# All 512 value columns of retention head 0 in the opening, in eight PSUM banks

## The chip, the cores and the metric

The kernel runs on one core of a Trainium2 chip. A core has TensorE (PE, matrix products into eight PSUM banks of 128 partitions by 512 float32), VectorE (DVE), ScalarE (ACT), GpSimd (POOL) and the queues that issue loads and stores (here mostly that of SyncE, SP). The metric is the device time of one execution in microseconds (us), the median of several runs. Before the change it was 1136.06 us, the median of three runs from 1134.89 to 1136.76.

## What is computed

One block of a hybrid model, for 512 tokens of width 1024: a normalised and modulated input `hmix` is projected by `w_in` into the inputs of two mixers (stick-breaking attention with 16 heads, retention with 4 heads), both are gated, projected and merged, and a gated feed-forward layer follows. What matters here is the beginning:

```python
mod = jnp.einsum('bd,de->be', c_act, w_ada[l]) + b_ada[l]
shift1, scale1, gate1, shift2, scale2, gate2 = jnp.split(mod, N_MOD, axis=-1)
hmix = modulate(rmsnorm(x, g_norm1[l]), shift1, scale1)
proj = jnp.einsum('bsd,de->bse', hmix, w_in[l])
sb_q, sb_k, sb_v, r_q, r_k, r_v, r_g, br = jnp.split(proj, IN_SPLITS, axis=-1)
...
rq = rotary(r_q.reshape(b, s_len, RET_HEADS, RET_QK_DIM))
rk = rotary(r_k.reshape(b, s_len, RET_HEADS, RET_QK_DIM)) * (RET_QK_DIM ** -0.5)
rv = r_v.reshape(b, s_len, RET_HEADS, RET_V_DIM)
o_ret = retention(rq.transpose(0, 2, 1, 3), rk.transpose(0, 2, 1, 3), rv.transpose(0, 2, 1, 3))
o_ret = head_rmsnorm(o_ret.transpose(0, 2, 1, 3)).reshape(b, s_len, RET_V_WIDTH)
o_ret = jax.nn.silu(r_g) * o_ret
```

A retention head has 256 query columns, 256 key columns, 512 value columns and 512 gate columns.

## The kernel before, in words

Products are made in three passes: every float32 operand is split into a high part (ScalarE copies it with rounding) and a low part (VectorE subtracts the high part), and a product is high by high, high by low and low by high, added up in one bank. `split` does this, `weight` loads a block of weights and splits it, `mm` (line 230) records every product, so nearly all rows of TensorE have that line.

The first part of the program, the **opening**, is written out in its order for PE, DVE and ACT; the queues and GpSimd stay with the scheduler, and so does everything between the opening and later written-out parts: there a scheduler with a cost model of its own puts instructions in order, and names (`ps_218`) are given anew at each build. The opening does this:

- `c` is activated and spread over all partitions by eight products (banks `z`); `keep_busy` issues products of a constant that nobody reads (`negones`, lines 456 to 464). The eight x tiles (128 rows of the width each) are squared, seven by ACT and one by DVE, and DVE adds squares 1 to 5 to square 0 (line 480). PE sums the columns of square 0 (with its additions), 6 and 7 in two halves of 256 tokens (`ssq`), and from these `rsqrt_rows` makes the factor r1, half by half.
- The modulation columns of tile n come from two loads of 512 KB (`sraw`), each multiplied by `cact` and summed by DVE (`dot`, line 391); the first shift column comes from PE (`dot_pe`). `h_t` (L429, DVE), `h_hi` (L435, ACT) and `h_lo` (L438, DVE) make the modulated tile n in high and low part.
- For tile n a `start` weight is loaded: its 128 rows, 256 query, 256 key and 256 value columns of head 0 (384 KB), split by `w_hi` (L418, ACT) and `w_lo` (L422, DVE). Tile 0 is multiplied unsplit, in plain float32 and in halves. Tiles 1 to 7 take 12 products of 512 columns for queries and keys (banks `ps` three times and `av`, with the weight as the stationary operand) and 12 of 256 columns for values (two blocks of 128 tokens share a bank `z`, so two banks).

After the opening `ret_qk` rotates queries and keys (L676 to L678, four reads of banks on DVE for each), `ret_v` splits the first half of the values, then `ret_scores` makes the scores from rotated queries and keys into three banks `z`; then `tok_proj` makes the other 256 value columns, with two weights of 512 KB and 96 products of 256 columns into two banks `ps`, and `ret_v` splits them. `ret_silu` makes the gate columns of head 0 with `tok_proj_wide`: four weights of 512 KB and 96 products of 512 columns into four banks `ps`. `ret_out` multiplies scores and values (30 products), squares the result, and `ret_gate` scales it and transposes it (L787). While this runs, DVE makes sums of the modulated tiles that later products need (`sv_acts`, L895 and L906).

The PSUM banks are four of the name `ps`, three `z` and one `av`. Weights have three buffers for what is loaded (`raw`), four for high parts (`whi`, of which `cact` holds one during the opening) and four for low parts (`wlo`).

## Time and profile before

| | |
|---|---|
| median of three runs | 1136.06 us (1134.89 to 1136.76) |
| the profiled execution | 1136.24 us, with a span of 1134.2 us from the first to the last instruction |
| PE busy | 1115.5 us, 98% of the span |
| DVE, ACT, GpSimd busy | 839.7, 554.6 and 55.3 us |
| first tile of the opening starts | 16.72 us |
| first product of the separate value half behind the opening | 53.41 us |
| gate columns of head 0, first to last product | 69.07 to 90.64 us |
| bytes moved, whole span | 190.92 MB |

The rows are read like this: start in us, duration in us, engine, source line, operation, what is written from what, shapes, count. In rows of the chain of waits only start, duration, engine, tile and line stand. Products overlap, so their durations are longer than the distance of their starts, and the distance is what counts for a sum. A plain float32 product leaves two records.

### The profile page before, as it was taken

To read this page: it belongs to the slowest core of one execution; us is meant where nothing else is said; L and a number is where in the kernel's file an instruction comes from. 1 tells how busy PE (TensorE), PEld (TensorE's weight loads), DVE (VectorE), ACT (ScalarE), POOL (GpSimd) and SP (SyncE) were. 2 spreads that over 40 slices of the span, in tenths; PEclk is the share of its full clock that TensorE was granted. 3 is DMA by queue.
4 is the path that set the end of the run, shared out by engine and by line. 5 is a ranking of instruction groups with operands and counts; after the bars stand their busy time and mean duration, and the time that the engine had idled before them with its cause. 6 is when DMAs were issued, how large, how long until landed. Compare 5 with 4: busy or idle time off the path is not lost.

```text
span 1134.2 us, 16143 instructions
## 1 busy us (share of the span) xinstructions
PE 1115.5 (98%) x6196; PEld 965.4 (85%) x6196; DVE 839.7 (74%) x1181; ACT 554.6 (49%) x869; POOL 55.3 (5%) x94
## 2 busy tenths in 40 slices
PE   8999999999999999999999999999999999999996
PEld 7888888888788888877878777889999999999986
DVE  7997846958977968377677756767997677677656
ACT  5445345445444645355565554357755444444333
POOL 0000000011021020000000000000000000000000
PEclk9999999999999999999999999999999999999998
DMA  9724341766776476866676348762565653565322
GB/s 352 281 75 149 130 130 60 234 134 204 241 167 206 152 157 226 219 193 180 170 203 169 119 139 279 264 186 56 150 185 152 184 168 107 148 181 141 93 75 75
DMA packets 63437, 190.92 MB, mean 168 GB/s; under 512 B 7809, under 2 KB 9857, under 8 KB 63361
## 3 DMA queue, kind: packets, MB, share of 16 engines
q1 hardware_dynamic: 56048, 171.02, 46.9%
q0 software_dynamic: 6768, 18.35, 9.5%
q8 instruction: 49, 0.80, 0.3%
q10 hardware_dynamic: 544, 0.52, 0.1%
q14 instruction: 28, 0.22, 0.1%
HBM read 146.35 MB, written 16.78 MB: 144 GB/s over the span
## 4 chain that ended last, share of the span: by engine, by line
PE 82%; DVE 7%; DMA 4%; ACT 4%; issue 2%; SPq 0%; DVEq 0%; ACTq 0%
PE ps L230 63%; PE z L230 14%; PE av L230 3%; DMA araw<-wada 3%; PE z L638 2%; DVE araw L258 2%; ACT s L622 1%; DVE wlo L876 1%; DVE wlo L210 1%; ACT g L825 1%; DVE t L783 0%; DMA t<-t 0%; PE z L787 0%; DMA o<-xT 0%; DVE s L211 0%
## 5 line engine op out<-in xcount | busy, mean ns | idle before, releaser
L230 PE MATMUL ps<-h,whi 128*128 128x512 f32 (+1 forms) x1154 | 340.0, 376 | 0.2
L230 PEld LDWEIGHTS ps<-h,whi 128*128 128x128 f32 x1154 | 208.1, 189 | 34.9 <-ACT h L435 1.6
L230 PE MATMUL ps<-h,wlo 128*128 128x512 f32 (+1 forms) x577 | 214.8, 376 | 0.0
L208 ACT ACTIVATE whi<-raw 128x1024 fp32r<-128x1024 f32 (+1 forms) x106 | 110.7, 1044 | 179.3 <-PE ps L230 127.7
L210 DVE TENSOR_TENSOR wlo<-raw,whi 128x1024 fp32r<-128x1024 f32 (+1 forms) x106 | 127.3, 1202 | 68.3 <-ACT whi L208 67.7
L230 PE MATMUL ps<-s,whi 128*128 128x512 f32 x480 | 148.7, 390 | 1.1 <-ACT s L208 0.9
L230 PEld LDWEIGHTS ps<-h,wlo 128*128 128x128 f32 x577 | 108.9, 189 | 17.2
L230 PE MATMUL z<-q,whi 128*128 128x256 f32 x504 | 106.8, 283 | 0.0
L230 PEld LDWEIGHTS ps<-s,whi 128*128 128x128 f32 x480 | 89.3, 188 | 19.8 <-ACT s L208 1.3
L876 DVE TENSOR_TENSOR wlo<-s,whi 128x1024 fp32r<-128x1024 f32 x46 | 56.3, 1225 | 53.8 <-ACT whi L872 53.7
L230 PE MATMUL ps<-s,wlo 128*128 128x512 f32 x240 | 93.4, 389 | 0.0
L230 PEld LDWEIGHTS z<-q,whi 128*128 128x128 f32 x504 | 84.9, 192 | 1.5
L230 PE MATMUL ps<-whi,h 128*128 128x512 f32 (+1 forms) x272 | 77.9, 365 | 0.0
L872 ACT ACTIVATE whi<-s 128x1024 fp32r<-128x1024 f32 x47 | 49.7, 1057 | 56.9 <-PE ps L230 41.8
L1185 DVE SCALAR_TENSOR_TENSOR o<-ps,mod,o 128x512 f32<-128x512 f32 (+1 forms) x63 | 42.4, 680 | 30.8 <-PE ps L230 30.8
L230 PEld LDWEIGHTS ps<-whi,h 128*128 128x128 f32 x272 | 49.2, 189 | 9.2 <-ACT t L1016 0.6
L210 DVE TENSOR_TENSOR s<-z,s 128x512 fp32r<-128x512 f32 (+1 forms) x60 | 33.6, 613 | 28.8 <-ACT s L208 28.8
L230 PEld LDWEIGHTS ps<-s,wlo 128*128 128x128 f32 x240 | 45.1, 188 | 9.4
L872 ACT ACTIVATE whi<-raw 128x1024 fp32r<-128x1024 f32 x28 | 29.6, 1058 | 43.9 <-PE ps L230 42.1
L230 PE MATMUL ps<-wlo,h 128*128 128x512 f32 (+1 forms) x136 | 49.5, 364 | 0.0
L230 PE MATMUL ps<-q,whi 128*128 128x256 f32 (+1 forms) x224 | 49.3, 314 | 0.0
L230 PE MATMUL z<-qp,whi 128*128 128x256 f32 x168 | 47.2, 283 | 0.0
(318 smaller groups left out, 2116.9 us busy)
## 6 DMA issues: line engine op xcount, KB each, us to landing
raw<-wp SPq DMA_DIRECT2D x139, 512.0 KB, 4.1
araw<-wada SPq DMA_DIRECT2D x32, 512.0 KB, 4.2
araw<-wp SPq DMA_DIRECT2D x30, 512.0 KB, 4.8
s<-wp SPq DMA_DIRECT2D x24, 512.0 KB, 5.8
sraw<-wada SPq DMA_DIRECT2D x16, 512.0 KB, 7.8
q<-qp SPq DMA_DIRECT2D x32, 256.0 KB, 3.7
spill<-o POOLq DMA_DIRECT2D x24, 256.0 KB, 4.7
o<-xT SPq DMA_DIRECT2D x16, 256.0 KB, 4.4
```

The costliest lines, as they stand in the source:

```text
L208: nc.scalar.activation(dst_hi, src, AF.Copy, scale=scale)
L210: return (eng or nc.vector).tensor_sub(dst_lo, src, f(dst_hi))
L230: return nc.tensor.matmul(o, lhs, rhs, start=start, stop=stop, skip_group_check=True).ins
L258: nc.vector.scalar_tensor_tensor(raw, raw, 1.0, cact, op0=ALU.mult, op1=ALU.mult, accum_out=col)
L622: nc.scalar.activation(t[:, at : at + w], z[bank][:, c : c + w], AF.Sigmoid, scale=scale)
L638: nc.tensor.transpose(at[bank][:, c : c + P], t[:, a + j * P : a + (j + 1) * P], ident)
L825: nc.scalar.activation(g, o, AF.Sigmoid, bias=sm[:, SM_BB + i : SM_BB + i + 1])
L872: nc.scalar.activation(hi, t, AF.Copy)
L876: nc.vector.tensor_sub(lo, t, f(hi))
L1185: return nc.vector.scalar_tensor_tensor(x1[d][:, hv], o[:, hv], mod[:, gcol + d : gcol + d + 1], x1[d][:, hv], op0=ALU.mult, op1=ALU.add,)
```

## The change

The `start` weights hold all 512 value columns, so a tile's values are 12 products of 512 columns into four banks: one `ps` and three `z`. With the four banks of queries and keys that makes eight. `tok_proj` with its two weights and 96 products is gone, and `ret_v` splits four whole banks. In the last tile the products are put bank by bank, values first. `keep_busy` issues 8 products instead of 16 at its first call. DVE adds squares 1 to 4 alone; PE sums square 5 with the others, as the first of four products in each half. `ret_scores` is called after `ret_v`.

```diff
--- before.py
+++ after.py
@@ -52,7 +52,7 @@
         return [(a, n)]
 
     for kt in range(KT):
-        add(("start", kt), "w_in", kt * P, 1, [(C_RQ, 256), (C_RK, 256), (C_RV, 256)])
+        add(("start", kt), "w_in", kt * P, 1, [(C_RQ, 256), (C_RK, 256), (C_RV, 512)])
     groups = [(("vg", h), (C_RV + h * RV, C_RG + h * RV)) for h in range(1, RH)] + [("sv", (C_V, C_V + 512))]
     for name, cols in groups:
         for half in range(2):
@@ -68,8 +68,6 @@
         for i in range(2):
             add(("rk", h, i), "w_in", 0, 8, rng(C_RK + h * RK + i * P, P))
         if h == 0:
-            for half in range(2):
-                add(("rv", 0, 1, half), "w_in", half * 512, 4, rng(C_RV + 256, 256))
             for part in range(4):
                 add(("rg", 0, part), "w_in", part * 256, 2, rng(C_RG, 512))
         for i in range(4):
@@ -373,10 +371,10 @@
         return res
 
     def start_weight(kt):
-        raw = load_raw(wp[WIDX[("start", kt)]], 768)
+        raw = load_raw(wp[WIDX[("start", kt)]], WCOLS)
         hi = wpool.tile([P, WCOLS], F32R, tag="whi", bufs=BUFS["whi"], name=nm("whi"))
         lo = wpool.tile([P, WCOLS], F32R, tag="wlo", bufs=BUFS["wlo"], name=nm("wlo"))
-        return raw[:, :768], hi[:, :768], lo[:, :768]
+        return raw, hi, lo
 
     raws, wts = {}, {}
     for kt in range(2):
@@ -463,7 +461,7 @@
             for _ in range(n):
                 mm(busy, negones, negones[:, 0:1].to_broadcast([P, S]), True, True)
 
-        keep_busy(16)
+        keep_busy(8)
 
         sq = {}
         for j in range(KT):
@@ -476,13 +474,13 @@
                 nc.vector.tensor_copy(cact[:, 0:S], cb[0])
             elif j == 6:
                 nc.scalar.activation(cact[:, S:], cb[1], AF.Copy)
-            if 0 < j < 6:
+            if 0 < j < 5:
                 nc.vector.tensor_add(sq[0], sq[0], sq[j])
         ssq = []
         for hv in HALVES:
             o = psz()[:, 0:256]
-            for j in (0, 6, 7):
-                mm(o, ones, sq[j][:, hv], j == 0, j == 7)
+            for j in (5, 0, 6, 7):
+                mm(o, ones, sq[j][:, hv], j == 5, j == 7)
             ssq.append(o)
         dot(0, 1)
         r1 = tmp()
@@ -499,17 +497,15 @@
         hs.append(pair("h"))
         w_hi(1)
         qk_ps = [ps() for _ in range(3)] + [psa()]
-        v_ps = [psz() for _ in range(2)]
-
-        def qk_products(w, act, hv, start=False, stop=False):
-            for i in range(4):
+        v_ps = [ps()] + [psz() for _ in range(3)]
+
+        def qk_products(w, act, hv, start=False, stop=False, banks=range(4)):
+            for i in banks:
                 mm(qk_ps[i][:, hv], w[:, i * P : (i + 1) * P], act[:, hv], start, stop)
 
         def v_products(act, w, blocks, start=False, stop=False):
             for b in blocks:
-                o = v_ps[b // 2][:, (b % 2) * 256 : (b % 2) * 256 + 256]
-                mm(o, act[:, b * P : (b + 1) * P], w[:, 512:768],
-                   start and b % 2 == 0, stop and b % 2 == 1)
+                mm(v_ps[b], act[:, b * P : (b + 1) * P], w[:, 512:], start, stop)
 
         for kt in range(KT):
             nx = kt + 1
@@ -528,6 +524,15 @@
                 for n, hv in enumerate(HALVES):
                     qk_products(raw, ts[0], hv, n == 0)
                     v_products(ts[0], raw, (2 * n, 2 * n + 1), True)
+            elif z:
+                for b in range(4):
+                    v_products(ah, hi, (b,))
+                    v_products(ah, lo, (b,))
+                    v_products(al, hi, (b,), False, True)
+                for i in range(4):
+                    qk_products(hi, ah, ALL, banks=(i,))
+                    qk_products(lo, ah, ALL, banks=(i,))
+                    qk_products(hi, al, ALL, False, True, banks=(i,))
             else:
                 qk_products(hi, ah, ALL)
                 qk_products(lo, ah, ALL)
@@ -681,20 +686,6 @@
                 res.append(hl)
         return res
 
-    def tok_proj(banks, ws):
-
-        for half in range(2):
-            hi, lo = weight(ws[half])
-            for k in range(4):
-                h = hs[half * 4 + k]
-                a, z = half == 0 and k == 0, half == 1 and k == 3
-                for b in range(4):
-                    c = slice(b * P, (b + 1) * P)
-                    o = banks[b // 2][:, (b % 2) * 256 : (b % 2) * 256 + 256]
-                    mm(o, h[:, 0, c], hi[:, k, :], a and b % 2 == 0, False)
-                    mm(o, h[:, 0, c], lo[:, k, :], False, False)
-                    mm(o, h[:, 1, c], hi[:, k, :], False, z and b % 2 == 1)
-
     def tok_proj_wide(banks, ws):
 
         for part, key in enumerate(ws):
@@ -708,18 +699,10 @@
                     mm(banks[b], h[:, 0, c], lo[:, k, :], False, False)
                     mm(banks[b], h[:, 1, c], hi[:, k, :], False, z)
 
-    def ret_v(h, first, between):
+    def ret_v(banks):
         vt = [pair("v") for _ in range(4)]
-        for i in range(2):
-            if i == 1:
-                between()
-            banks = first if i == 0 else [ps(), ps()]
-            if i == 1:
-                tok_proj(banks, [("rv", h, i, half) for half in range(2)])
-            for b in range(4):
-                c = slice(i * 256, (i + 1) * 256)
-                split(vt[b][:, 0, c], vt[b][:, 1, c],
-                      banks[b // 2][:, (b % 2) * 256 : (b % 2) * 256 + 256])
+        for t, o in zip(vt, banks):
+            split(t[:, 0, :], t[:, 1, :], o)
         return vt
 
     def ret_scores(h, qk):
@@ -1059,8 +1042,8 @@
         store(0, 1, p1)
 
     qk = ret_qk(0, qk_ps)
-    st = {}
-    vt = ret_v(0, v_ps, lambda: st.update(ret_scores(0, qk)))
+    vt = ret_v(v_ps)
+    st = ret_scores(0, qk)
     sgs = ret_silu(0)
     steps = sv_acts()
     sacts = next(steps)
```

What this makes of the order of instructions, at three places. First PE ahead of the first tile. Before (`negones` are the products that nobody reads, `z` from `ones` the column sums, `mod` by `sraw` the first shift column):

```order
L230 MATMUL ps_132<-negones 128x512 x16
L230 MATMUL z_172<-t_149,ones 128x256
L230 MATMUL z_172<-t_167,ones 128x256
L230 MATMUL z_172<-t_170,ones 128x256
L230 MATMUL z_176<-t_149,ones 128x256
L230 MATMUL z_176<-t_167,ones 128x256
L230 MATMUL z_176<-t_170,ones 128x256
L230 MATMUL ps_183<-mod,sraw_100 128x1 x8
```

and now (`t_156` is square 5, `t_141` the sum of squares, `t_158` and `t_161` squares 6 and 7):

```order
L228 MATMUL ps_132<-negones 128x512 x8
L228 MATMUL z_163<-t_156,ones 128x256
L228 MATMUL z_163<-t_141,ones 128x256
L228 MATMUL z_163<-t_158,ones 128x256
L228 MATMUL z_163<-t_161,ones 128x256
L228 MATMUL z_168<-t_156,ones 128x256
L228 MATMUL z_168<-t_141,ones 128x256
L228 MATMUL z_168<-t_158,ones 128x256
L228 MATMUL z_168<-t_161,ones 128x256
L228 MATMUL ps_176<-mod,sraw_100 128x1 x8
```

Eight idle products are gone, and each half has a product of square 5 ahead of the sum.

Second, PE where the opening ends. Before, the last rows of tile 7 (queries and keys in `ps_218` to `av_221`, values in `z_222` and `z_223`) and the first of the separate value half (`ps_654`):

```order
L230 MATMUL ps_220<-h_530,whi_452 128x512
L230 MATMUL av_221<-h_530,whi_452 128x512
L230 MATMUL z_222<-whi_452,h_530 128x256 x2
L230 MATMUL z_223<-whi_452,h_530 128x256 x2
L230 MATMUL ps_654<-wlo_659,h_216 128x256
L230 MATMUL ps_654<-whi_658,h_216 128x256 x2
```

and now, with gate columns (`ps_649` to `ps_652`) behind the last bank of the opening:

```order
L228 MATMUL av_214<-h_525,whi_447 128x512
L228 MATMUL av_214<-h_525,wlo_448 128x512
L228 MATMUL av_214<-h_525,whi_447 128x512
L228 MATMUL ps_649<-whi_655,h_209 128x512
L228 MATMUL ps_649<-wlo_656,h_209 128x512
L228 MATMUL ps_649<-whi_655,h_209 128x512
L228 MATMUL ps_650<-whi_655,h_209 128x512
L228 MATMUL ps_650<-wlo_656,h_209 128x512
L228 MATMUL ps_650<-whi_655,h_209 128x512
L228 MATMUL ps_649<-whi_655,h_250 128x512
L228 MATMUL ps_651<-whi_655,h_209 128x512
```

The gate products moved up to the end of the opening. `ps_649` is the bank that held the values of the first block of tokens (`ps_215`); `ps_650`, `ps_651` and `ps_652` (its first product stands 21 products behind the end of the opening) are the banks of queries and keys `ps_211`, `ps_212` and `ps_213`. The three score banks are the value banks `z_216` to `z_218`; the first scoring product stands 29 products behind the end of the opening.

Third, DVE at the same place. Before (`wlo_713` is the second weight of the separate value half, `t` from `ps` and the table are the steps of the rotation):

```order
L210 TENSOR_TENSOR wlo_713<-raw_710,whi_712 128x1024
L676 TENSOR_TENSOR t_564<-ps_218,table_559 128x512
L677 TENSOR_TENSOR t_565<-ps_219,table_559 128x512
L676 TENSOR_TENSOR t_572<-ps_218,table_559 128x512
L678 TENSOR_TENSOR t_564<-t_564,t_565 128x512
L677 TENSOR_TENSOR t_573<-ps_219,table_559 128x512
```

and now (`wlo_686` is the second gate weight, `v_591` and `v_592` the values of the first two blocks):

```order
L208 TENSOR_TENSOR wlo_686<-raw_683,whi_685 128x1024
L208 TENSOR_TENSOR v_591<-ps_215,v_591 128x512
L208 TENSOR_TENSOR v_592<-z_216,v_592 128x512
L681 TENSOR_TENSOR t_559<-ps_211,table_554 128x512
L682 TENSOR_TENSOR t_560<-ps_212,table_554 128x512
L681 TENSOR_TENSOR t_567<-ps_211,table_554 128x512
L683 TENSOR_TENSOR t_559<-t_559,t_560 128x512
L682 TENSOR_TENSOR t_568<-ps_212,table_554 128x512
L681 TENSOR_TENSOR t_575<-ps_213,table_554 128x512
L208 TENSOR_TENSOR q_564<-t_559,q_564 128x512
L683 TENSOR_TENSOR t_567<-t_567,t_568 128x512
L682 TENSOR_TENSOR t_576<-av_214,table_554 128x512
```

Two value splits moved ahead of the rotation; `ps_211` is read for the last time by `t_567`, `ps_212` by `t_568`, and `ps_213` by the step that follows the last row here. The high part of the second gate weight (`whi_685`, ACT) goes into a buffer that tile 6 reads to its end.

## The prediction

> **What bounds the kernel now.** I read the page's shares first, then the chain of work that ended last from 0 to 110 us, then the timelines of TensorE, VectorE and ScalarE around the opening.
>
> ```profile
> PE 1115.5 (98%) x6196; PEld 965.4 (85%) x6196; DVE 839.7 (74%) x1181; ACT 554.6 (49%) x869; POOL 55.3 (5%) x94
> ```
>
> TensorE (PE) is busy for 98% of the span, so nearly every product added or removed moves the end. The exceptions are stretches where PE waits for others; the opening has two. Behind the first fourteenth of PE's list (about 115 us) its order is the same before and after, so I cost only what lies before it. The chain, start and length in us:
>
> ```profile
> 9.76 0.69 DVE t L480
> 10.55 0.70 DVE t L480
> 11.29 2.86 PE z L230 x12
> 16.72 1.56 PE ps L230 x6
> 18.72 0.86 PE z L230 x4
> 22.18 0.96 PE ps L230 x3
> 23.38 0.69 PE ps L230 x3
> 24.07 0.23 PE av L230
> 24.30 0.95 PE z L230 x8
> 26.18 0.47 PE z L230 x4
> ```
>
> Up to 11.25 VectorE's running sum of squares (L480) sets the pace, then the column sums on PE (z, x12), then the tiles. From 22.18 on come the tiles 1 to 7. In one a 512-column product takes 0.23 us (0.92 for four) and a 256-column value product 0.118 us (1.42 for twelve). But the first group of a tile takes 0.96 instead of 0.69: PE waits. For whom:
>
> ```profile
> PEld ps L230 <- ACT h L435: 1.6, 6, 0.4
> 21.29 1.22 DVE L391 SCALAR_TENSOR_TENSOR sraw<-sraw,cact 128x1024 f32<-128x1024 f32 x1
> 24.24 0.95 DVE L422 TENSOR_TENSOR wlo<-raw,whi 128x768 fp32r<-128x768 f32 x1
> 25.11 0.75 DVE L429 SCALAR_TENSOR_TENSOR t<-o,sm,t 128x512 f32<-128x512 f32 x1
> 25.78 1.22 DVE L391 SCALAR_TENSOR_TENSOR sraw<-sraw,cact 128x1024 f32<-128x1024 f32 x1
> ```
>
> VectorE works without a gap: L391 of one tile begins at 21.29, that of the next at 25.78, also 4.49 us. So the tiles repeat every 4.49 us and are paced by VectorE, whose last step of a tile (L429) releases ScalarE's h, which releases PE.
>
> **The change part by part.** *The start.* One add of 0.74 us (9.76 to 10.55 is the pitch with its overlap) leaves the chain to the column sums; its square becomes two more PE products of 0.43 us (two value products of that width and type take 0.86, row 18.72).
>
> ```profile
> 7.16 4.00 PE L230 MATMUL ps<-negones 128*128 128x512 f32 x16
> 10.55 0.62 ACT L474 ACTIVATE t<-o 128x512 f32<-128x512 f32 x1
> 12.89 0.47 ACT L324 ACTIVATE t<-z,eps 128x256 f32<-128x256 f32 x1 [1.72 <-PE z L230]
> 13.99 1.84 PE L230 MATMUL ps<-mod,sraw 128*128 128x1 f32 x16
> 15.87 0.26 ACT L407 ACTIVATE sm<-ps,sm 128x1 f32<-128x1 f32 x1 [0.76 <-PE ps L230]
> 16.16 0.51 ACT L498 ACTIVATE t<-t,sm 128x256 f32<-128x256 f32 x1
> ```
>
> The idle products end near 11.16, just before the column sums; with eight (0.25 us each) they end near 9.2, so they do not hold the sums, and their removal alone is worth nothing: the work that covers it is VectorE's chain. The sum of squares is ready at 10.5; PE then runs squares 0, 6, 7 (the last is ready at 11.17) to 11.85 and the second half to 13.57, where six of them from 11.29 ended at 13.87. Behind it stand the modulation product (13.99), ScalarE's L407 and L498, and the first tile. VectorE's half comes 0.74 earlier, so the PE path decides: 0.3 us. **−0.3**; ends 0 and −0.74.
>
> *The first tile* runs plain f32: two value products (x4 records) take 0.86, so 0.43 each at 256 columns and 0.86 at 512. Four of them: +1.72. The wait of 0.18 before 22.18 is gone, because h is ready near 21.6 and the tile now ends near 23.4. **+1.54**.
>
> *Tiles 1 to 7.* Each has 24 products of 512 columns. The nearest rows for the wide form are the 96 gate products of the same shape, which run from 69.07 to 90.64:
>
> ```profile
> 53.41 0.28 PE L230 MATMUL ps<-wlo,h 128*128 128x256 f32 x1
> 69.07 0.40 PE L230 MATMUL ps<-wlo,h 128*128 128x512 f32 x1
> 90.64 4.24 PE L230 MATMUL z<-v,s 128*128 128x512 f32 x18
> 48.20 1.23 DVE L210 TENSOR_TENSOR wlo<-raw,whi 128x1024 fp32r<-128x1024 f32 x1
> 49.33 0.76 DVE L438 SCALAR_TENSOR_TENSOR h<-t,sm,h 128x512 fp32r<-128x512 f32 x1
> ```
>
> That is 0.225 us each; the tile's own rows say 0.23. At 0.228 a tile takes 5.47 and seven take 38.3. Before, 22.18 to 53.41 is 31.23. **+7.07**; ends +6.6 (0.225) and +7.4 (0.23). VectorE's step for the low half of the weight grows from a pitch of 0.87 (24.24 to 25.11) to 1.13 (48.20 to 49.33), so its tile is 4.75, under 5.47: VectorE no longer sets the pace, and its lead over PE, near 1.8 us at tile 1, grows by 0.7 a tile. Its longer step costs nothing under that cover; without it the tiles would take at least 4.75. The loads grow to 1.57 MB a tile:
>
> ```profile
> 4.50:36.00 31.50, 31.13 (x160) 26.38 (x159) 27.67 (x47) 16.66 (x33) 0.00 (x0) 1.00 1.03 398
> ```
>
> At 398 GB/s that is 3.95 us. The weight of tile 2 is the tightest: three larger loads shift it by 0.39 MB, one microsecond, to about 22, when ScalarE gets to it; PE needs it only near 29. Cost 0.
>
> *The 96 separate products go*, with two weight loads, their splits and the eight half-bank splits. Between 53.41 and 69.07, 15.66 us, stand 95 of them and 24 scoring products:
>
> ```profile
> 53.57 7.49 PE ps L230 x62
> 61.06 0.38 PE z L230 x2
> 62.15 0.12 PE z L230
> 63.11 3.49 PE z L230 x21
> ```
>
> 62 take 7.49, 0.121 each: 95 are 11.5. The scoring products keep their 3.99 and now stand among gate products. **−11.5**; ends −11.3 and −11.7 (15.66 less 3.99).
>
> *The seam.* All eight banks are now held at the end of the opening, near 61.7; I call it E. Gate products need them back one by one. VectorE's rope steps free three:
>
> ```profile
> 52.44 0.69 DVE L676 TENSOR_TENSOR t<-ps,table 128x512 f32<-128x512 f32 x1 [0.61 <-PE ps L230]
> 53.05 0.68 DVE L677 TENSOR_TENSOR t<-ps,table 128x512 f32<-128x512 f32 x1
> 53.65 1.05 ACT L208 ACTIVATE whi<-raw 128x1024 fp32r<-128x1024 f32 x1
> ```
>
> A step takes 0.60. The last tile closes the value banks first. The split of the second gate weight (ScalarE 1.05, then VectorE 1.13) has to wait for a buffer until tile 6 ends near E−5; behind it VectorE splits the first two value banks, and is done near E−1.55. Rope then begins and, in the order shown above, frees the first three query and key banks at E+0.3, E+1.5 and E+4.5. PE asks for them at E+0.7, E+1.6 and E+4.8 (three, seven and 21 products of 0.228). The first gate bank is a value bank, long free. The scoring products come at E+6.6, their rotated key at E+6.3. Behind a waiting gate product everything on PE queues. I take **+0.1**; ends 0 and +2, because the margins are 0.1 to 0.4.
>
> *The head's own wait.*
>
> ```profile
> 97.44 0.62 PE L230 MATMUL ps<-h,whi 128*128 128x512 f32 x2
> 101.02 2.07 DVE L783 SCALAR_TENSOR_TENSOR t<-z,sm,t 128x512 f32<-128x512 f32 x3
> 101.83 0.33 PE L787 MATMUL z<-con,t 128*128 128x128 f32 x1 [0.37 <-DVE t L783]
> ```
>
> The transposes waited 0.37 behind 17 products; in the new order 26 stand before them, 2.0 us more cover. **−0.2**, ends 0 and −0.4.
>
> Sum: −0.3 + 1.54 + 7.07 − 11.5 + 0.1 − 0.2 = −3.3. The profiled execution took 1136.24 (span 1134.2 and 2.04 around it), 0.18 over the median of 1136.06, so **1132.8** stands against the median.
>
> **The rivals.** *The banks come back late* (0.20). For it: eight banks, three releases with 0.1 to 0.4 us of margin, and a VectorE list in which one weight split takes 1.13. Against: both the first gate bank and the scoring banks are value banks that close 2.7 to 4.8 us before E. A slip of one such split passes through at about 1.0, two at 2.1: −2.3 to −1.2, near **1134.3**. The Trainium skill (Trainium Kernel Development and Optimization, Best Practices) warns to mind PSUM pressure, since emptying banks does not speed up with the products; that is this rival, and no row of before shows all eight held.
>
> *The clock falls back* (0.05), the case on the other side.
>
> ```profile
> 3.76 3.75 PE L230 MATMUL z<-con,mod 128*128 128x128 f32 x16 [3.76 <-DVE mod L454]
> ```
>
> Its sixteen records start over 3.40 us (3.76 to 7.16), 0.21 each for 128 columns; later 256 columns take as long. So PE ran at half rate for its first 3.4 us of work, though the granted clock in the row from 4.50 on reads 1.00. With eight idle products gone, PE has gaps of about 0.4 and 0.5 us between 9.2 and 10.5. If it stayed at half rate through sums (3.4 more) and modulation (1.7 more) and needed 3.4 us of the first tile to recover (1.7 more), it loses 6.8: +3.5, **1139.6**. It decides once 5.6 us are lost, that is from half a microsecond's loss in the first tile on. The Trainium skill (TensorE: Matmul & The Clock Gate, Part 1: The HAM clock gate) has full rate begin after a busy window of about 3.4 us and end after an idle one as long. By that rule gaps of 0.5 us change nothing and the sum stays; the first 3.4 us of the trace agree with it, its second half no row here shows.
>
> *The opening becomes bound by its loads* (0.03): it decides below 288 GB/s (1.57 MB in 5.47 us). At the 245 of the next stretch a tile is 6.4: +6.6, so +3.3, **1139.4**.
>
> ```profile
> 36.00:54.00 18.00, 17.94 (x103) 15.42 (x101) 17.39 (x26) 8.85 (x17) 0.00 (x0) 1.00 0.75 245
> ```
>
> Against it: there the engines moved data for only 0.75 of the time, and while they had work throughout (1.03 before it) they held 398.
>
> **How the numbers follow.** The forecast, −3.3 as summed, has 0.72; its own range is 1131.6 to 1133.9, from the ends of the terms and the spread of the runs (1134.89 to 1136.76). With the rivals I give 1131.3 to 1135.2: the bank case lies inside, the clock and load cases outside. About 0.2%, 2.3 us, is what a measurement here can tell from no change. The forecast's gain passes it with 0.87 (0.63), the bank case with 0.25 (0.05): faster 0.68. Within 0.2%: 0.09 and 0.15, so 0.24. Slower: the two last cases, 0.08.
>
> **What would show it.** The first tile should start near 16.4, tile 1 near 23.4 with no wait on ScalarE's h, and tiles repeat every 5.47; PE's last opening product should end near 61.7, the gate products with the scoring ones near 87.6 instead of 90.64, and the transposes should stand without a wait. A tile above 5.6 would make the third term wrong; idle PE before a gate bank's first product, released by a rope step, would make it the bank case; records of 0.43 for 256 columns after 9.2, the clock. It is wrong altogether if the ends of the head's work near 91 do not carry through to the last instruction.

## The result

The changed kernel took 1130.80 us, the median of six runs (1130.07 to 1132.12), against 1137.18 for six runs of the kernel before on the same chip (1134.89 to 1140.32). The ratio is 0.9949, with a 95% interval of 0.9932 to 0.9965: 5.8 us. In two later comparisons it was 0.9968 (0.9953 to 0.9982, 3.6 us) and, with two unread weight blocks left in the packed array, 0.9960 (0.9943 to 0.9976, 4.5 us). The forecast was 3.3. So the direction was right and the size is 0.3 to 2.5 us beyond the forecast, depending on the comparison; the first median lies 0.5 under the range that I gave, the later one of the same kernel (1132.35) inside it.

The profiled execution took 1131.71 us with a span of 1129.8 (before: 1136.24 and 1134.2). The page's shares:

```profile
PE 1112.0 (98%) x6096; PEld 958.7 (85%) x6096; DVE 837.8 (74%) x1174; ACT 554.1 (49%) x863; POOL 65.9 (6%) x94
```

There are a hundred records of matrix products fewer, and GpSimd (POOL) busier by 10.6 us, though it runs the same 94 instructions. That second number had no place in my sum. The chain of waits of the changed kernel, start and length (rows between these are left out):

```profile
16.04 1.56 PE ps L228 x6
23.19 0.69 PE ps L228 x3
32.30 0.68 PE ps L228 x3
37.74 0.68 PE ps L228 x3
61.32 6.59 PE ps L228 x29
70.63 2.60 PE z L228 x16
75.83 12.95 POOL s L592 x2
88.82 3.92 PE z L228 x16
95.46 5.90 PE ps L228 x26
```

The first tile starts at 16.04 (before: 16.72), tile 1 at 23.19, and the tiles repeat every 5.44 us (32.30 to 37.74). The opening ends at 61.32, and the gate products follow at once: the chain stays on TensorE (PE), the row of waits for ScalarE's h is gone, and no bank comes back late. Up to here it is what the sum says. Then a GpSimd row stands on the chain for 12.95 us, at the causal selects of head 0's scores (the line is L587 in the kernel before), and the products of scores and values resume at 88.82. TensorE's waits from 80 to 110 us in the changed kernel, the engine and line waited for, total, times and longest:

```profile
PE z L228 <- POOL s L592: 1.4, 1, 1.4
```

A ledger shows where the time went. Each number is the start of the same instruction of TensorE (the last row is the whole span), as a mean over three executions with a trace: of the kernel before (the one shown, experiments 5 and 10) and of the changed kernel (the one shown, experiment 6, and experiment 11, whose instructions are the same over another layout of the weights).

| place | before | after | difference | forecast |
|---|---|---|---|---|
| first tile | 17.03 | 16.06 | −0.97 | −0.3 |
| first product of scores and values, head 0 | 90.95 | 86.86 | −4.09 | −3.1 |
| a product of the next projection (117.76 in the trace before) | 118.05 | 114.64 | −3.41 | −3.3 |
| behind the transposes of head 2 (294.53 there) | 294.05 | 290.08 | −3.97 | −3.3 |
| last but one product | 1123.93 | 1119.89 | −4.04 | −3.3 |
| span | 1133.82 | 1129.43 | −4.40 | −3.3 |

At 115 us the forecast is met to 0.1, but by two errors that cancel: about 1.0 more gained in front of the scores, 0.7 lost again behind them. Another 0.6 comes at head 2, and 0.36 behind the last product, where the program's closing synchronisation is shorter (from VectorE's last instruction to the end 4.03 us before, 3.66 after). The experiments ask for these one by one.

### The profile page after: what moved, and what is told of

It reads as the page before. It is cut to its first block, busy times and chain, and to the rows that moved or that the text cites. A ratio compares the mean times of both kernels' runs of the same rounds, so it can differ in the third digit from the quotient of the medians.

```text
span 1129.8 us, 15925 instructions
## 1 busy us (share of the span) xinstructions
PE 1112.0 (98%) x6096; PEld 958.7 (85%) x6096; DVE 837.8 (74%) x1174; ACT 554.1 (49%) x863; POOL 65.9 (6%) x94
## 4 chain that ended last, share of the span: by engine, by line
PE 86%; DVE 5%; ACT 3%; DMA 3%; issue 2%; POOL 1%; SPq 0%; DVEq 0%; ACTq 0%
PE ps L228 65%; PE z L228 15%; PE av L228 3%; PE z L643 2%; ACT s L627 1%; POOL s L592 1%; DMA araw<-wada 1%; DVE araw L256 1%; DMA sraw<-wada 1%; ACT g L808 1%; DVE wlo L859 1%; DVE wlo L208 0%; DMA q<-qp 0%; DVE t L766 0%; DMA t<-t 0%
## 5 line engine op out<-in xcount | busy, mean ns | idle before, releaser
L208 DVE TENSOR_TENSOR wlo<-raw,whi 128x1024 fp32r<-128x1024 f32 (+1 forms) x104 | 125.0, 1203 | 72.8 <-ACT whi L206 72.0
L228 PE MATMUL ps<-whi,h 128*128 128x512 f32 x222 | 71.4, 391 | 0.0
L228 PEld LDWEIGHTS ps<-whi,h 128*128 128x128 f32 x222 | 41.6, 188 | 9.5 <-ACT t L999 0.6
L228 PE MATMUL z<-q,wlo 128*128 128x256 f32 x168 | 46.4, 283 | 0.0
```

The source lines that it names most:

```text
L208: return (eng or nc.vector).tensor_sub(dst_lo, src, f(dst_hi))
L228: return nc.tensor.matmul(o, lhs, rhs, start=start, stop=stop, skip_group_check=True).ins
```

## Experiments

### The start: which of the two edits carries it

The prediction gave the moved square 0.3 us and the eight idle products nothing.

Experiment 1, the start edits alone on the kernel before:

```diff
-        keep_busy(16)
+        keep_busy(8)
...
-            if 0 < j < 6:
+            if 0 < j < 5:
...
-            for j in (0, 6, 7):
+            for j in (5, 0, 6, 7):
```

> The kernel before with the start edits alone: eight idle products instead of sixteen, and square 5 summed by TensorE instead of VectorE. Values, tiles and everything behind are as before. Theory 1 (the first tile starts earlier because VectorE's chain to the column sums is one add shorter, and the gain passes through the tiles, since VectorE's own work is shorter too): first tile at 16.0 to 16.1 instead of 16.72, and the last instruction 0.5 to 0.7 us earlier. Theory 2 (the sum on record, -0.3: TensorE's two extra products eat more than half): first tile near 16.4, end 0.3 earlier. Rival (the start is hidden behind the loads of tile 2): first tile early, tile 2 as before, end 0.0. A difference of 0.7 us is under what the times resolve (about 0.2%, 2.3 us); it is read from the trace.

Experiment 7, the idle products alone on the kernel before:

```diff
-        keep_busy(16)
+        keep_busy(8)
```

> The kernel before with eight idle products instead of sixteen and nothing else. Prediction's step (their removal alone is worth nothing, VectorE's five adds hold the column sums until 11.2): column sums start at 11.2 to 11.3 and the first tile near 16.7, as before, less the x loads' own spread of some tenths; records of 256 float32 columns stay at 0.43 us. Rival (the clock falls back in the 2 us of idle TensorE that this leaves before the sums): records of 0.8 us after 9.2, and a first tile past 18.

Experiment 9, the moved square without the shorter run of idle products, on the changed kernel:

```diff
-        keep_busy(8)
+        keep_busy(16)
```

> The changed kernel with sixteen idle products instead of eight, so that of the start edits only the moved square is left. Theory S (the two start edits work together: with VectorE's chain shorter by one add, sixteen idle products end after it and hold the column sums): idle products end between 11.0 and 12.0, the column sums start there instead of 9.3 to 10.4 and have sixteen records (3.4 us), so the first tile starts at 16.9 to 17.9, 0.9 to 1.9 later than in the changed kernel and later than in the kernel before. Rival (the moved square alone carries the gain): first tile at 16.0 to 16.3.

Experiment 1 ran at 0.999 of the kernel before (0.998 to 0.9999). Its first tile started at 15.83; experiment 7's at 16.35, experiment 9's at 16.88. TensorE's records at the start of 1 and, below the dots, VectorE's (DVE) last adds and TensorE's records of 7, from their timelines:

```profile
9.65 3.62 PE L230 MATMUL z<-t,ones 128*128 128x256 f32 x16
15.83 1.56 PE L230 MATMUL ps<-t,raw 128*128 128x256 f32 x6
...
9.39 1.48 DVE L480 TENSOR_TENSOR t<-t,t 128x512 f32<-128x512 f32 x2
6.98 2.42 PE L230 MATMUL ps<-negones 128*128 128x512 f32 x8
10.93 2.86 PE L230 MATMUL z<-t,ones 128*128 128x256 f32 x12 [1.52 <-DVE t L480]
```

In experiment 7 TensorE is idle for 1.52 us until VectorE's last add is done (9.39 and 1.48 give 10.87), and the column sums start at 10.93. That is the prediction's step as it was put. But it needs the idle products to be done by then, and they are not always. Experiment 5 is the kernel before once more, without an edit, for a second trace; its timelines of VectorE and TensorE follow the expectation:

> The kernel before once more, for a second execution with a trace. Theory D1 (TensorE's waits behind 115 us come from loads that land later or earlier from one execution to the next): the transposes of head 2, which waited 1.5 us for VectorE in the first trace of this kernel, wait a different time here (anything from 0 to 1.5 us), and other waits between 380 and 740 us differ by some tenths. Theory D2 (the head-2 wait belongs to the kernel before, and the change takes it away): 1.2 us or more again.

```profile
9.14 1.48 DVE L480 TENSOR_TENSOR t<-t,t 128x512 f32<-128x512 f32 x2
6.98 5.06 PE L230 MATMUL ps<-negones 128*128 128x512 f32 x16
11.88 2.75 PE L230 MATMUL z<-t,ones 128*128 128x256 f32 x12
17.20 1.56 PE L230 MATMUL ps<-t,raw 128*128 128x256 f32 x6
```

Here VectorE is done at 10.62, and the sums start at 11.88, behind the sixteen idle products, which took 5.06 us instead of 4.00. In the execution that I had read they ended at 11.16 and VectorE at 11.24, a margin of 0.08 by the ends of the records (up to 0.16 more by the moment at which the next product can start: here 11.88, with the record's end at 12.04), and the row names only the one that came last. Experiment 10, a third execution of the kernel before without an edit, did as 5: idle products 4.83 us long, first tile at 17.16.

> A third execution of the kernel before with a trace. If the start hangs on which comes last, VectorE's adds or the idle products, the first tile starts between 16.4 and 17.2 again. If the late modulation loads of head 2 belong to this kernel, its transposes wait 0.5 us or more for VectorE; by chance alone anything from 0 to 1.5.

What differs between the executions is when TensorE comes to full rate. An idle product takes 0.43 us at first and 0.22 later, and the step falls at 7.7 in the trace before, at 9.4 in experiment 10, at 9.7 in 5, and in other executions anywhere from 7.1 to 9.7. The later it is, the longer sixteen of them last; the eight of the changed kernel end before 10.2 in all of its executions. The Trainium skill (TensorE: Matmul & The Clock Gate, Part 1: The HAM clock gate) says that the window behind the step runs freely and does not start with the kernel, so that the step varies by 500 ns to either side; here it moved over 2.6 us.

Over the executions with a trace the first tile started at 16.63 to 17.20 with sixteen idle products in four executions with the original start (the trace before, experiments 2, 5 and 10), and at 15.83 to 16.36 in the seven with both edits (the changed kernel's, 1, 3, 4, 6, 8, 11). The moved square alone does not bring that, as experiment 9 shows: with sixteen idle products the sums start behind these, at 10.70, though VectorE is done at 10.16. The shorter run alone came to 16.35 in experiment 7, the late end of that range; one execution does not tell how much the square adds to it.

In the changed kernel a delay behind the start is carried on one to one: experiment 12 below, with twenty-four idle products, moved the first tile by 3.64 us and the products of scores and values by 3.66. In the kernel before it is not quite so. From the first tile to the first product of scores and values experiment 1 took 73.49 us, where the other executions with narrow values took 73.91 to 73.92. That fits its theory 1, by which VectorE's shorter list helps the tiles too. The earlier end that it expected did not come: waits late in the program, told below, hide it in this trace.

Experiment 9 also showed the clock falling back, which I had as a rival with 0.05. Its records, and the granted clock (the third number from the right) in stretches of half a microsecond, start and end first:

```profile
7.12 3.74 PE L228 MATMUL ps<-negones 128*128 128x512 f32 x16
16.88 2.51 PE L228 MATMUL ps<-t,raw 128*128 128x256 f32 x6
17.00:17.50 0.50, 0.50 (x3) 0.39 (x4) 0.50 (x2) 0.18 (x1) 0.00 (x0) 0.85 1.03 410
17.50:18.00 0.50, 0.50 (x3) 0.41 (x2) 0.50 (x1) 0.50 (x2) 0.00 (x0) 0.50 1.03 410
...
20.50:21.00 0.50, 0.50 (x2) 0.17 (x1) 0.50 (x2) 0.00 (x0) 0.00 (x0) 0.73 1.03 410
```

From about 17.3 to 20.7 TensorE ran at half the clock, though it was busy throughout. Up to the products of scores and values that execution lost 1.66 us beside its later start (72.46 us from the first tile, 70.80 in the changed kernel's three). It is the execution in which full rate came earliest, at 7.1 with the first idle product (experiment 8: 7.2, without a fall), three times 3.4 us before the fall. In front of the fall stand sixteen one-column products, three idle ones and a gap of 0.1 us; that such a stretch counts as idle when a window falls exactly on it is my reading. No experiment was made for it, but the end of the traces bears on it, where the clock falls as well. In experiment 5 (same columns as above):

```profile
1122.43:1125.85 3.42, 1.35 (x5) 0.87 (x5) 2.88 (x9) 2.16 (x6) 0.00 (x0) 1.00 0.62 207
1125.85:1127.00 1.15, 0.00 (x0) 0.00 (x0) 1.12 (x3) 0.00 (x0) 0.00 (x0) 0.50 0.20 70
```

The last 3.4 us before that fall hold five records of products, 1.35 us of TensorE's time. So the stretch in front of a fall need not be empty; how much work it may hold stays open. By the Trainium skill's rule (same page and part) the rate falls after an idle window of about 3.4 us; no such idle time is in this trace, so there the measurement stands against the rule as I had used it.

### The wide values alone

Experiment 2 is the changed kernel with the start edits undone (the first diff above, backwards).

> The changed kernel with the start edits undone (sixteen idle products, five squares added by VectorE), so the 512 value columns, the last tile bank by bank and the removal of the separate products alone. Theory 1 (nearly all of the gain is TensorE work: 11.5 removed, 6.9 + 1.5 added): first tile at 16.7, gate and score products ahead of the kernel before by 3.1 instead of 3.8 us, and a time near 1131.5 (about 0.4% under the kernel before, 0.7 us over the changed kernel). Rival (the start edits carry more than their 0.7 us, because a longer run of idle products shifts the clock or VectorE's lead): tiles 1 to 7 no longer at 5.44 us, or a time within 2 us of the kernel before.

Measured: a ratio of 0.9969 (0.9956 to 0.9982), 3.5 us, with the first tile at 16.63. From the first tile to the first product of scores and values it takes 70.81 us, as the changed kernel does (70.80), and the kernel before 73.91 to 73.92 in its three executions. So the tiles, the dropped products and the seam are worth 3.1 us whatever the start does; the sum had 1.54 + 7.07 − 11.5 + 0.1 = −2.8. The start adds its own share on top.

### The order of the last tile

Experiment 3 closes all eight banks at the end of the last tile, as the other tiles' order does:

```diff
-            elif z:
-                for b in range(4):
...
-                    qk_products(hi, al, ALL, False, True, banks=(i,))
             else:
```

> The changed kernel with the last tile in the order of the other tiles (all banks closed in the last eight products) instead of bank by bank. Theory 1 (the bank-by-bank order is what keeps the seam free): the rope steps start 1 us or so later against the tile's end, TensorE waits at the first or second gate bank for a rope step, 0.4 to 1.2 us, and the wait is carried on: 0.4 to 1.2 us over the changed kernel. Rival (VectorE's lead is enough without it, or the scheduler fills the gap with other products): no wait, time as the changed kernel within 0.3 us in the trace. Second rival (the bank case of the prediction comes true here): 2 us or more between the last tile and the scores' end.

From its first tile to the products of scores and values it took 71.54 us against 70.80: 0.74 more. The wait, from the view of waits (55 to 92 us), VectorE's timeline and the chain:

```profile
PE ps L228 <- ACT v L206: 0.5, 1, 0.5
...
60.09 0.69 DVE L672 TENSOR_TENSOR t<-ps,table 128x512 f32<-128x512 f32 x1 [1.53 <-PE ps L228]
61.29 0.68 DVE L672 TENSOR_TENSOR t<-ps,table 128x512 f32<-128x512 f32 x1
...
62.12 9.12 PE ps L228 x39
```

VectorE stands idle for 1.53 us until the first query bank closes, and its third rope step (61.29 to 61.97) is the last to read that bank. The first gate product writes into it and starts at 62.12. The row of waits names ScalarE's v, of which a record ends at 62.08, but in the program no gate product here waits for v. In the changed kernel the first gate bank is a value bank, emptied long before, and rope runs from 59.35. So theory 1 holds in its mechanism and its size: it is the bank rival of the prediction, called up by the old order, at 0.7 instead of the 1.0 that I gave a slip. The times (ratio 0.9963, 0.9949 to 0.9977) do not resolve it.

### GpSimd's selects beside VectorE's sums

In the changed kernel the scores come later than the work that VectorE fills its time with, the sums of modulated tiles (`sv_acts`, now L878). The group of the selects on GpSimd from 74 to 90 us (count, shortest, median and longest in ns, first and last start), and VectorE's timeline beside it:

```profile
L592 POOL TENSOR_SCALAR_AFFINE_SELECT s<-s x8: 287/298/12691, 74.3 to 89.0; 128x128 fp32r<-128x128 f32 x6, 128x256 fp32r<-128x256 f32 x2
...
76.08 1.08 DVE L878 TENSOR_TENSOR s<-h 128x256 f32<-128x256 f32 x3
77.08 2.77 DVE L878 TENSOR_TENSOR s<-s,h 128x256 f32<-128x256 f32 x8
...
86.26 2.36 DVE L208 TENSOR_TENSOR wlo<-raw,whi 128x1024 fp32r<-128x1024 f32 x2
89.38 1.23 DVE L889 TENSOR_TENSOR q<-s,q 128x1024 fp32r<-128x1024 f32 x1 [0.76 <-ACT q L888]
```

Seven selects take 0.3 to 0.5 us. One starts at 76.08, together with the first of thirty VectorE instructions that follow each other without a gap and read two operands from SBUF, and ends at 88.77, in the 0.76 us in which VectorE waits for ScalarE. In the kernel before the same selects ran between 66.66 and 69.22, mostly beside VectorE's splits of scores, which read one operand from a bank.

Experiment 4 puts the sums behind one-column copies that need the selects' results; experiment 8 is the same kernel with more rounds, and experiment 6 the changed kernel beside it:

```diff
     steps = sv_acts()
     sacts = next(steps)
-    for _ in steps:
-        pass
+    seen = small(6)
+    for n in range(6):
+        done = nc.vector.tensor_copy(seen[:, n : n + 1], f(st[n // 2][:, n % 2, 0:1]))
+    with tc.issue_after(done.ins):
+        for _ in steps:
+            pass
```

> The changed kernel, where VectorE's sums of the modulated tiles (sv_acts) are put behind six one-column copies that read the masked scores, so that they cannot start before GpSimd's eight selects are done. TensorE's order is the same. Theory C (the selects are slow only because VectorE's sums of two SBUF operands run beside them): the eight selects take 2 to 3 us instead of 14.94, TensorE's three waits for them (3.8 us in all, 1.5 of it lost against the kernel before) are gone, the products of scores and values start near 87 instead of 88.8, and the kernel ends 1.2 to 1.6 us before the changed one (about 1129.4), unless VectorE, which now idles 3 us, is late for something behind. Rival 1 (the selects are slow for another reason, such as their place behind the gate weights' splits): they take 10 us or more still, and VectorE loses that time too. Rival 2 (selects fast, but the 1.4 us are lost again at the head's own scaling and transposes): products at 87, transposes wait 1 us or more, no gain at the end.

> The changed kernel once more, timed beside the kernel before. Theory C (a select of GpSimd that meets VectorE's run of sums is shut out until the run ends, in some executions and not in others): the times fall into two groups, one near 1130.1 and one 1.3 to 1.5 us above, and the trace shows either 2 to 4 us for the eight selects and no wait of TensorE for them, or 13 to 15 us and a wait of about 1.4. Rival (the selects are always slow in this kernel, and the spread of the times comes from loads alone): 13 to 15 us again, times spread without a gap.

> The changed kernel with VectorE's sums behind the selects, as before in this study, now timed in more rounds beside the changed kernel. Theory C: no execution loses the 1.4 us, so the median is 0.3 to 1.0 us under that of the changed kernel, near 1130.3, and the lowest times of both are the same within 0.3 us. Rival (the held sums cost VectorE as much later as they save): the medians agree within 0.3 us, or this one is higher.

GpSimd and VectorE in experiment 4, then GpSimd in experiment 6:

```profile
74.25 2.34 POOL L592 TENSOR_SCALAR_AFFINE_SELECT s<-s 128x256 fp32r<-128x256 f32 x8 [72.77 <-DVE s L209]
75.89 0.89 DVE L1052 COPY sm<-s 128x1 f32<-128x1 f32 x6
76.69 1.42 DVE L878 TENSOR_TENSOR s<-h 128x256 f32<-128x256 f32 x4
...
74.28 14.94 POOL L592 TENSOR_SCALAR_AFFINE_SELECT s<-s 128x256 fp32r<-128x256 f32 x8 [72.80 <-DVE s L209]
```

With the sums 0.6 us later (76.69 instead of 76.08) the selects take 2.34 us instead of 14.94, and again 2.35 in experiment 8; TensorE's wait is gone in both. From the first tile to the ledger's product near 115 us both take 98.00 us, against 98.97 and 98.98 in the two executions of the changed kernel with long selects, 0.97 less, and 97.79 to 97.81 in experiments 11 and 2, where the selects were quick without it. This is shown: where the selects are shut out, it is the sums that do it. The Trainium skill (SBUF — State Buffer, Who interferes with whom) says that a VectorE instruction with two SBUF inputs contends with a GpSimd instruction that reads SBUF, and that the pair of ports they share is an exclusive lock. The trace agrees that one of them is blocked; here it stayed blocked through thirty VectorE instructions in a row.

It does not happen in every execution. Of the five with the sums where the change has them (the trace shown, 6, 9, 11 and 12) four had 14.94 us, and experiment 11 had 3.18. Experiments 2 and 3, where the same selects and sums also met, had 3.18 and 3.79. There the selects went through between the adds, one by one. What decides it was not found. My expectation that the times would fall into two groups was wrong: experiment 6 ran from 1131.02 to 1135.35 without a gap.

Nor did the times settle whether the held sums pay. Experiment 4 had a median of 1130.46 (ratio 0.9948, 0.9932 to 0.9965); timed together, experiment 8 had 1132.00 (0.9957, 0.9942 to 0.9972) and experiment 6 1132.35 (0.9968, 0.9953 to 0.9982). The microsecond is in the trace; in the times it is under what these runs tell apart.

### The late part: head 2 and the loads

In the kernel before the transposes of head 2 waited 1.5 us for VectorE at 291.80, and in the changed kernel not at all. The chain of the kernel before there, and its waits from 270 to 295 us:

```profile
262.62 4.81 DMA araw<-wada
267.46 1.23 DVE araw L258 x2
291.08 0.67 DVE t L783
PE z L787 <- DVE t L783: 1.5, 1, 1.5
```

VectorE is late because it waited for a load of modulation columns, 4.81 us long. By the same row the wait was 0.2 and 0.3 us in experiments 5 and 10, 1.6 in experiment 7. So most of the 1.5 is that one execution's, and theory D1 of experiment 5 (loads land differently) is right as far as it goes. But all five executions with narrow values waited (experiment 1: 0.7), and the changed kernel's three did not. Nor does it belong to the narrow values alone: of the wide ones experiment 3 waited 0.2 and experiment 9 0.4. Two experiments looked for a cause. Experiment 11 keeps the two old weight blocks in the packed array, so that all later weights lie where they did:

```diff
         if h == 0:
+            for half in range(2):
+                add(("rv", 0, 1, half), "w_in", half * 512, 4, rng(C_RV + 256, 256))
             for part in range(4):
```

> The changed kernel with the two weight blocks of the old value half kept in the packed weight array, but not loaded: every later block lies at the same address as in the kernel before, and the program is otherwise the changed one. Theory L (the modulation loads behind 250 us land later in the kernel before because the packed array lies otherwise): the last of the eight modulation products of head 2 comes 24.7 us or more behind the same reference product of TensorE and its transposes wait 0.5 us or more. Rival (no link with the layout): 23 to 24.2 us and a wait under 0.1, as in every execution of the changed kernel so far.

No wait at all: theory L falls. Its time was 1132.30, ratio 0.9960. Experiment 12 puts the changed kernel as late as the kernel before:

```diff
-        keep_busy(8)
+        keep_busy(24)
```

> The changed kernel with twenty-four idle products instead of eight, which puts everything behind them some 3 us later and changes nothing else. In the traces so far the transposes of head 2 waited 0.07 to 1.5 us for VectorE in the five executions of kernels with the narrow values, and in the one wide kernel that ran as late as those (sixteen idle products, 0.3); in the seven earlier wide ones 0.06 at most. Theory T (what decides is how late the program stands against something that does not shift with it): first tile at 18.5 to 20, and a wait of 0.2 us or more at head 2. Rival (it belongs to the narrow kernels, or is chance): a wait under 0.1, as in the other wide kernels.

```profile
7.01 6.65 PE L228 MATMUL ps<-negones 128*128 128x512 f32 x24
19.68 1.56 PE L228 MATMUL ps<-t,raw 128*128 128x256 f32 x6
PE z L770 <- DVE t L766: 0.2, 1, 0.2
```

It took 1136.13 us in its one run, with the first tile at 19.68 as expected, and 0.2 of a wait at head 2 by the row (280 to 300 us), 0.07 by the distance of the products around it. That lies on the line between the two theories, and decides nothing. Whether the 0.56 us of the ledger at this place belong to the change stays open.

Much of the rest of the spread is transfers as well. Near 695 us products wait in every trace, 0.4 to 1.6 us; in the chains of the trace before and of experiments 2, 10 and 11 a DMA of 4.3 to 5.3 us (`t<-t`) stands in front. Near 735 they wait for a weight, up to 0.9 us, and near 385 up to 0.3 us for VectorE, each in some executions and not in others. Experiment 1 had all three, and its profiled execution ended 0.7 us behind that of the kernel before in spite of a start 0.89 earlier.

## Why the prediction came out as it did

Its sign and its main terms were right, and each shows in the rows that it named.

- **The start**, −0.3. Measured −0.68 between the two traces shown, −0.97 over three each. In the two traces shown VectorE decides both times, as the prediction had it. Its last add before ends at 11.24, and the first tile starts 5.48 us behind it (experiment 7 has 5.48 too). After, the last add is this row of its timeline:

```profile
9.44 0.68 DVE L478 TENSOR_TENSOR t<-t,t 128x512 f32<-128x512 f32 x1
```

It ends at 10.12, 1.12 earlier, for the add that is gone and for other landings of x; and the first tile stands 5.92 behind it, 0.44 more, for the two products that came in. The step that failed is "their removal alone is worth nothing: the work that covers it is VectorE's chain". The cover was 0.1 to 0.2 us thick in the one execution that I read and is not there in two others of the same kernel, since the run of idle products lasts 4.0 to 5.1 us. At 5.48 behind VectorE's last adds (10.62 and 11.54) the first tile would have come at 16.10 and 17.02 in experiments 5 and 10, not at 17.20 and 17.16: by this estimate the idle products cost 0.4 of the 0.97 on average. I had quoted the half rate of the first 3.4 us without asking when it ends in another run. The end of −0.74 that I gave was no bound, for it was VectorE's alone.
- **The first tile**, +1.54. Measured 7.15 us (16.04 to 23.19) against 5.46 before (16.72 to 22.18): +1.69.
- **Tiles 1 to 7**, +7.07. Measured 38.13 against 31.23: +6.90, a tile 5.45 where 5.47 was forecast, and no wait for h. VectorE's longer steps cost nothing, as argued.
- **The separate products and the seam**, −11.5 and +0.1. Measured 25.52 us from the end of the opening to the first product of scores and values (61.32 to 86.84), against 37.23 before (53.41 to 90.64): −11.71. The seam cost nothing. The three rope steps that free the query and key banks:

```profile
60.60 0.68 DVE L681 TENSOR_TENSOR t<-ps,table 128x512 f32<-128x512 f32 x1
61.80 0.68 DVE L682 TENSOR_TENSOR t<-ps,table 128x512 f32<-128x512 f32 x1
64.80 0.68 DVE L681 TENSOR_TENSOR t<-ps,table 128x512 f32<-128x512 f32 x1
```

They end at 61.28, 62.48 and 65.48, and the gate products that need the banks start at 61.83, 62.74 and near 65.9: 0.3 to 0.6 us to spare, where the prediction had 0.1 to 0.4. Experiment 3 shows what the bank-by-bank order is for: 0.74 us.
- **The head's own wait**, −0.2. Measured −0.13 where the selects were quick (experiment 11: 20.86 us from the tenth product into the last bank of scores and values to the ledger's product at 117.76, 20.99 before; 20.77 to 21.07 in experiments 2, 3, 4 and 8). But in front of it stands a wait that the sum did not have. The prediction followed the moved steps on TensorE, VectorE and ScalarE, and never on GpSimd. The scores move from 61 to 68 us, and their selects with them, from beside splits into the stretch of VectorE's sums; 1.4 us of waiting, 1.7 by the distance of the products, in most executions. Where it falls, 0.5 of it comes back at the transposes, which then wait less (20.39 instead of 20.86).
- **The rivals.** The banks came back in time; the old order of the last tile would have brought that rival. The loads did not bind the tiles, at 5.44 us each. The clock never fell back in the executions of the two kernels compared, and once in a variant.
- **The carrying through.** The lead of 3.4 us at 115 us stands at 4.0 behind the last product. What I had named as the thing that would prove it wrong did not happen.

The range was too narrow on the fast side. It was built on a spread of three runs (1134.89 to 1136.76), while the 55 runs of the kernel before that were timed beside the change and the experiments ran from 1133.85 to 1141.97. The three comparisons of the change give −3.6, −4.5 and −5.8 us with intervals of nearly 2 to either side, and the traces −4.4; of what lies beyond the forecast there, 0.7 is the start, 0.3 the tiles and products, 0.4 the closing and 0.6 the open wait at head 2, against which the selects cost 1.1 on average and give 0.2 back.

## What to carry over

When two causes release the same wait, one trace shows only the one that came last; where they lie some tenths of a microsecond apart, cost the edit as if either could be in front, and ask how each varies from run to run. When a step moves in time, look up what runs beside it at its new place on every engine that shares something with it, GpSimd beside VectorE above all. A lead that is gained near the start of a kernel bound by TensorE carries through to the end, and is read more sharply from the distance between two products in a trace than from medians.

## What was not expected of the hardware

- One GpSimd select of about 0.3 us took 12.69 us beside thirty VectorE instructions in a row with two SBUF operands. In experiments 2 and 11 the eight selects and the sums interleaved, and the eight took 3.18.
- TensorE's step to full rate moved between 7.1 and 9.7 us after the start over fourteen executions, with its first product at 3.55 to 3.77 in all of them. In the one with the earliest step the granted clock fell to 0.50 from about 17.3 to 20.7 while TensorE was busy, behind 3.4 us of which half went to one-column products.
